# A two-layer hybrid block: the attention of a layer as a pipeline of steps, with the remaining merge-gate products cut in quarters and spread over the steps

## The chip, the core and the metric

One core of one Trainium2 chip runs the whole program. The metric is the device time of one execution in microseconds (us). The kernel before took 3766.13 us (median of three runs, 3756.99 to 3768.46). TensorE (PE) does the matrix products, VectorE (DVE) and ScalarE (ACT) the elementwise work, and the queue of SyncE (SP) issues nearly all DMAs.

## What is computed

Two layers over 1024 latent and 256 context tokens of width 1024. Each layer normalises the tokens, multiplies them by a wide input matrix, and feeds three mixers: a recurrence (branch A), a short convolution (B) and a differential attention (C). Their outputs are merged with sigmoid gates that are themselves products of the normalised input (`g_merge`). Cut to what matters here:

```python
def diff_attend(q, k, v, lam):                       # 4 heads, two 64-wide maps per head
    s = einsum('bqhcd,bkhcd->bhcqk', q, k) * (64 ** -0.5)
    p = softmax(s, axis=-1)
    attn = p[:, :, 0] - lam * p[:, :, 1]
    return einsum('bhqk,bkhv->bqhv', attn, v)

def merge_branches(y_a, y_b, y_c, z_a, z_b, z_c, g_merge, w_branch, w_out):
    y = stack([y_a * silu(z_a), y_b * silu(z_b), y_c * silu(z_c)], axis=-2)
    br = einsum('btiw,iwd->btid', y, w_branch)
    gates = sigmoid(g_merge.reshape(..., 3, 1024))
    return sum(gates * br, axis=-2) @ w_out
```

Latent queries read all 1280 keys, context queries only the 256 of the context. The last layer does not need the context's outputs, so there it has no context queries and no context gates.

## The kernel before

All products of projections are made in three parts of split precision: every operand is a high and a low half (`hT0h` and `hT0l` for the normalised tokens, `whi` and `wlo` for a weight block), and one term is three matmuls (`mm3`, L155). A *group* (`cm_group`, L165) is eight terms, so 24 matmuls into one PSUM tile `pjt`, for 128 output channels and 512 (or, for the context, 256) tokens.

A layer runs these stages in program order: the projections; the recurrence (`rwkv_stage`, L583; 20 chunks, each a serial chain of small products with DVE and ACT work between); the attention (`attn_stage`, L835); the branch products and the merge (`branch_stage`, L930); the output product. Three generators hold projection work that is not needed at once and serves as filling for PE: `vd_fill` (L795), `z_fill` (L806) and `g_fill` (L820), the last making the merge gates: 72 groups in layer 0 and 48 in layer 1, each followed by a tanh on ACT (`fth`) and a store (`th`). `fill` (L1143) is called 63 times in the recurrence, three times in a chunk and three ahead of them. `PACE` (L27) says in which of these calls one group is made: in each in layer 0, in two of three in layer 1. After the 29 and 26 groups of the first two generators, 38 gate groups are left in layer 0 and 32 in layer 1 when the recurrence ends. The program writes them behind the attention.

The order on each engine isn't that of the program. A list scheduler with a cost model places the instructions when the kernel is built, takes what is ready and comes first in the program, and takes later work where an engine would stand idle. So the gate groups written behind the attention lie between its instructions. On the chip each engine then works through its list in that fixed order.

The attention works on 128 queries at a time (`e` in 0, 1 of a block of 256, `qb`). Such a step makes scores `s` for two maps (six PSUM tiles from a pool of four), takes maxima on DVE (`mx`, L894) and exponentials on ACT (`p`, L903), scales and subtracts the second map (L911, L912), turns the result on PE (`at`, ten transposes, L918) and splits it into `ath` and `atl`. After two steps 30 matmuls make the output `o` of the block, which is copied (`oy`) and stored. Layer 0 has 40 steps (8 of them of context queries, with two key tiles in place of ten), layer 1 has 32.

`branch_stage` starts with the products of branch B: their operand `yb` (`yraw`, L1029) and their accumulators `acc` (loaded from the stored gates, L1044) lie in the buffers of `hT` (`bigh`, `bigl`), so they come free with the last gate group. Its other buffers (`bp`) lie where those of the attention were. The chain `y_a` (L946: loads `ra` and `rb`, then `pc`, `st`, logarithm, exponential, split into `ya`) must end before branch A's products on that token group. In layer 0 all products of the branches rotate over two more PSUM tiles (`PJB`, L26), which lie where the attention's were; in layer 1 only from the last of B's four weight blocks on.

Of the kernel before, what the change touches and what calls it, by code (L numbers as in the profile page):

```python
# [26 lines left out]
PACE = ((1, 1), (2, 3))  # L27
# [12 lines left out]
def tile_backbone(ctx: ExitStack, tc: tile.TileContext, xT_in, cond_in, w_mod, vecs, w_in, d_up, a_up,  # L40
# [114 lines left out]
    def mm3(ps, terms):  # L155
# [7 lines left out]
        return i.ins  # L163

    def cm_group(w, j, mov, t0, n):  # L165
        ps = pj_tile()
        terms = []
        for k in range(4 * len(w)):
            hi, lo = w[k // 4]
            s = slice(128 * j, 128 * j + 128)  # L170
            terms.append(((hi[:, k % 4, s], lo[:, k % 4, s]),
                          tok(mov, k, t0, n) if isinstance(mov, dict) else
                          (mov[0][:, k, t0:t0 + n], mov[1][:, k, t0:t0 + n])))
        run_late(mm3(ps[:, :n], terms))
# [620 lines left out]
    def vd_fill(l, b, sp):  # L795
# [6 lines left out]
        for i0 in range(0, 10, 2):  # L802
            tm_block(w, [i0], cb)
# [16 lines left out]
    def g_fill(l, sp):  # L820
        gq = GROUPS[l < NL - 1]
        for i in range(3):
            for b in range(4):
# [4 lines left out]
                for j, (t0, n) in jg:  # L828
                    p = cm_group(w, j, hT[0], t0, n)
# [5 lines left out]
    def attn_stage(l):  # L835
# [16 lines left out]
        for h in range(4):  # L852
            kd = []
            for c in range(2):
# [6 lines left out]
                kd.append((kh, kl))  # L861
            vh = ap.tile([128, 10, 128], F32R, tag="vh", name="vh")
# [5 lines left out]
            for qb in range(5 if full else 4):  # L868
                q0 = 256 * qb
                key0 = TL if q0 >= TL else 0  # L870
                nk = T - key0
                chunks = [(c, min(512, T - c)) for c in range(key0, T, 512)]
                nkt = nk // 128
                qraw = ap.tile([128, 2, 256], F32, tag="qraw", name="qraw", bufs=1)
                for c in range(2):
                    for e in range(2):
                        dma.dma_start(out=qraw[64 * e:64 * e + 64, c, :], in_=q_dr[l][h][64 * c:64 * c + 64, q0:q0 + 256])
                qs = ap.tile([128, 2, 256], F32R, tag="qs", name="qs", bufs=2)
                se.copy(out=qs, in_=qraw)
                ve.tensor_tensor(out=qs[64:128], in0=qraw[64:128], in1=qs[64:128], op=ALU.subtract)  # L880
# [379 lines left out]
```

## Time and profile before

| | us |
|---|---|
| median of three runs | 3766.13 |
| the profiled execution, as timed | 3755.48 |
| its span, first to last instruction | 3753.7 |
| PE busy | 3550.3 (95%) |
| DVE busy | 2403.3 (64%) |
| ACT busy | 1720.9 (46%) |
| mean granted TensorE clock | 0.977 |

A busy PE can be full, or it can be slow: matmuls overlap, and a matmul at half clock counts as busy for longer. So the number of matmuls in a stretch and the granted clock are read beside the busy time, and the stages are looked at one by one. The three lines of the program's timeline that matter here are the recurrence (747 to 1257 us in layer 0, 2605 to 3077 in layer 1), the attention (1272 to 1699 and 3092 to 3498), and the start of the branch stage after it.

### The profile page before, as it was taken

What the parts mean: (1) busy time and instruction counts of PE and PEld (TensorE: products, weight loads), DVE (VectorE), ACT (ScalarE), POOL (GpSimd) and SP (SyncE); (2) the same over time, 40 slices, a digit from 0 to 9 for tenths busy, and PEclk for the clock granted to TensorE, in tenths of its full rate; (3) what the DMA queues carried; (4) which work ended last, traced back from release to release, by engine and by line L of the source; (5) the groups of instructions that cost most, each with busy time, mean ns of one, the idle gap of its engine ahead of it and who ended that gap; (6) DMA issues with size and microseconds to landing.
All of it is one profiled execution on the core that took longest, in us unless ns stands there. A gap on an engine that the chain in (4) does not pass through costs nothing. (4 is left out here: it accounts for less than half of the span.)

```text
span 3753.7 us, 71161 instructions
## 1 busy us (share of the span) xinstructions
PE 3550.3 (95%) x28540; PEld 2917.8 (78%) x28540; DVE 2403.3 (64%) x5128; ACT 1720.9 (46%) x3295; POOL 82.9 (2%) x252
## 2 busy tenths in 40 slices
PE   7999999999999999968899999999999999999699
PEld 5788988888888788855776778988878778887377
DVE  6746733387777477765655766633898857778472
ACT  5644211144444477754434763212444436776440
POOL 0100000000000000000000110000000000000000
PEclk9999999999999999978999999999999999999799
DMA  5545222333332322405663455222333333233373
GB/s 203 143 129 157 77 95 94 132 105 106 116 107 99 103 89 86 151 21 171 212 199 128 117 156 157 80 96 93 106 112 119 114 94 100 84 98 100 129 244 124
DMA packets 378571, 454.75 MB, mean 121 GB/s; under 512 B 119808, under 2 KB 266752, under 8 KB 378240
## 3 DMA queue, kind: packets, MB, share of 16 engines
q1 hardware_dynamic: 376320, 447.58, 37.4%
q8 instruction: 224, 3.67, 0.4%
q0 software_dynamic: 1920, 2.62, 0.4%
q14 instruction: 107, 0.88, 0.1%
HBM read 300.66 MB, written 146.80 MB: 119 GB/s over the span
## 5 line engine op out<-in xcount | busy, mean ns | idle before, releaser
L160 PE MATMUL pjt<-hT0h,whi 128*128 128x512 f32 x1488 | 552.6, 372 | 3.6 <-ACT hT0h L292 1.4
L160 PE MATMUL pjt<-hT0l,whi 128*128 128x512 f32 x1488 | 536.4, 361 | 1.1 <-DVE hT0l L293 0.9
L160 PE MATMUL pjt<-hT0h,wlo 128*128 128x512 f32 x1488 | 530.9, 357 | 0.1
L160 PE MATMUL pjt<-hT1h,whi 128*128 128x512 f32 (+1 forms) x1072 | 422.3, 394 | 4.2 <-ACT tl L327 1.6
L160 PE MATMUL pjt<-hT1l,whi 128*128 128x512 f32 (+1 forms) x1072 | 417.0, 389 | 0.0
L160 PE MATMUL pjt<-hT1h,wlo 128*128 128x512 f32 (+1 forms) x1072 | 414.0, 386 | 1.3 <-DVE wlo L116 1.3
L115 ACT CAST whi<-wraw 128x1024 fp32r<-128x1024 f32 x208 | 217.2, 1049 | 301.0 <-PE pjt L160 274.2
L116 DVE TENSOR_TENSOR wlo<-wraw,whi 128x1024 fp32r<-128x1024 f32 x208 | 254.7, 1228 | 144.9 <-ACT whi L115 142.7
L160 PEld LDWEIGHTS pjt<-hT0h,whi 128*128 128x128 f32 x1488 | 283.0, 190 | 57.7 <-issue 10.2
L160 PEld LDWEIGHTS pjt<-hT0l,whi 128*128 128x128 f32 x1488 | 283.3, 190 | 43.9 <-issue 4.9
L160 PEld LDWEIGHTS pjt<-hT0h,wlo 128*128 128x128 f32 x1488 | 282.5, 190 | 42.4 <-issue 1.5
L903 ACT ACTIVATE p<-s,mx 128x512 f32<-128x512 f32 (+1 forms) x400 | 240.0, 610 | 90.1 <-DVE mx L898 84.8
L894 DVE TENSOR_REDUCE mx<-s 128x1 f32<-128x512 f32 (+1 forms) x400 | 228.1, 588 | 73.8 <-PE s L892 72.4
L160 PEld LDWEIGHTS pjt<-hT1h,whi 128*128 128x128 f32 x1072 | 202.0, 188 | 51.8 <-issue 7.3
L160 PEld LDWEIGHTS pjt<-hT1h,wlo 128*128 128x128 f32 x1072 | 201.9, 188 | 42.9 <-DVE wlo L116 2.8
L160 PEld LDWEIGHTS pjt<-hT1l,whi 128*128 128x128 f32 x1072 | 202.0, 188 | 41.8 <-issue 5.0
L892 PE MATMUL s<-kh,qs 128*128 128x512 f32 (+1 forms) x400 | 156.5, 397 | 38.6 <-ACT p L903 34.6
L645 ACT COPY dg<-mb 32x128 f32<-32x128 f32 x320 | 94.7, 296 | 161.8 <-DVE mb L639 143.6
L160 PE MATMUL pjt<-ya,whi 128*128 128x512 f32 (+1 forms) x448 | 144.1, 406 | 15.2 <-ACT ya L115 13.3
L892 PE MATMUL s<-kl,qs 128*128 128x512 f32 (+1 forms) x400 | 148.0, 375 | 1.2 <-DVE kl L116 1.2
L695 DVE TENSOR_TENSOR P<-at,R 128x16 f32<-128x16 f32 (+6 forms) x280 | 137.7, 492 | 9.0
L697 DVE TENSOR_REDUCE R<-P 128x4 f32<-128x16 f32 (+6 forms) x280 | 136.3, 487 | 8.6
(270 smaller groups left out, 7889.2 us busy)
## 6 DMA issues: line engine op xcount, KB each, us to landing
wraw<-in_w_in_dram SPq DMA_DIRECT2D x148, 512.0 KB, 3.9
kr<-kr SPq DMA_DIRECT2D x68, 512.0 KB, 4.4
wm<-in_w_mod_dram SPq DMA_DIRECT2D x48, 512.0 KB, 3.7
th<-fth SPq DMA_DIRECT2D x96, 256.0 KB, 2.1
wraw<-in_w_br_dram SPq DMA_DIRECT2D x36, 512.0 KB, 4.5
th<-th SPq DMA_DIRECT2D x64, 256.0 KB, 3.9
wraw<-in_w_out_dram SPq DMA_DIRECT2D x24, 512.0 KB, 4.3
bk<-bkt SPq DMA_DIRECT2D x80, 128.0 KB, 2.4
```

Of the source, the lines that this page charges most:

```text
L115: se.copy(out=hi, in_=src)
L116: ve.tensor_tensor(out=lo, in0=src, in1=hi, op=ALU.subtract)
L160: i = te.matmul(out=ps, lhsT=a, rhs=b, start=(c == 0), stop=(c == n - 1))
L645: se.copy(out=dg[s, d], in_=mb[s, d, p, :, 32 * q:32 * q + 32])
L695: ve.tensor_tensor(out=pv, in0=at[:, i0:i1, i1:32].unsqueeze(2).to_broadcast([128, 4, nm, n]), in1=R[:, b + 1:8, i1:32].unsqueeze(1).to_br ...
L697: ve.tensor_reduce(out=R[:, b + 1:8, i0:i1].rearrange("p m i -> p i m"), in_=pv, axis=AX.X, op=ALU.add)
L892: te.matmul(out=s[:, :n], lhsT=qs[:, c, 128 * e:128 * e + 128], rhs=kd[c][x][:, c0:c0 + n], start=(x == 0), stop=(x == 1))
L894: ve.tensor_reduce(out=mx[:, x0:x0 + 1], in_=s[:, :n], axis=AX.X, op=ALU.max)
L903: se.activation(out=p[:, o:o + n], in_=tiles[x0][:, :n], func=AF.Exp, scale=0.125, bias=mx[:, 3:4], accum_out=sums[:, x0:x0 + 1])
```

## The change

The attention is written as a pipeline of steps. In step x the scores and exponentials of step x's queries stand ahead of the turning of those of step x-1, and the output product of a block comes in the step after its second half was turned. The generators yield after each quarter of a group (`mm3_steps`), and the attention calls `fill(x, part)` twice in each step, which makes as many quarters as bring the total to an even share: 184 quarters over 41 slots in layer 0, 128 over 33 in layer 1. `PACE` in layer 0 goes from every turn of the recurrence to seven of eight, so 55 groups are made there in place of 63, and 46 gate groups are left for the attention in place of 38. In layer 1 the share stays at two of three, with other turns left out, and 32 groups remain as before.

```diff
-PACE = ((1, 1), (2, 3))
+PACE = ((7, 8, 46), (2, 3, 32))
...
+    def mm3_steps(ps, terms, step):
...
+            if c % (3 * step) == 0 and c < n:
+                yield
         last_mm[0] = i.ins
...
+    def cm_steps(w, j, mov, t0, n):
+
+        ps = pj_tile()
+        yield from mm3_steps(ps[:, :n], list(cm_terms(w, j, mov, t0, n)), 2)
+        run_late(last_mm[0])
+        yield ps[:, :n]
...
-                    p = cm_group(w, j, hT[0], t0, n)
+                    for p in cm_steps(w, j, hT[0], t0, n):
+                        if p is None:
+                            yield
...
-    def attn_stage(l):
+    def attn_stage(l, fill):
...
+        nq = 5 if full else 4
+        steps = [(h, qb, e) for h in range(4) for qb in range(nq) for e in range(2)]
+        kd = vd = qs = prev = done = None
+        for x, (h, qb, e) in enumerate(steps + [(0, 0, 0)]):
+            last = x == len(steps)
+            if not last:
+                if qb == 0 and e == 0:
+                    kd = keys(h)
+                if e == 0:
+                    qs = queries(h, qb)
+                sm = softmax(kd, qs, qb, e)
+                next(sm)
+            fill(x, 0)
+            if not last:
+                pr = next(sm)
+            if done is not None:
+                product(*done)
+                done = None
+            if prev is not None:
+                pp, ph, pq, pe = prev
+                if pe == 0:
+                    if pq == 0:
+                        vd = values(ph)
+                    at = [ap.tile([128, 10, 256], F32R, tag=t, name=t, bufs=1) for t in ("ath", "atl")]
+                turn(pp, at, pq, pe, 0)
+                fill(x, 1)
+                turn(pp, at, pq, pe, 1)
+                if pe == 1:
+                    done = (ph, pq, vd, at)
+            if not last:
+                prev = (pr, h, qb, e)
+        product(*done)
...
-        paced = itertools.count()
+        turns = itertools.count()
 
         def fill():
 
-            if next(paced) % PACE[l][1] < PACE[l][0]:
-                next(both, None)
+            x = next(turns)
+            if (x + 1) * PACE[l][0] // PACE[l][1] > x * PACE[l][0] // PACE[l][1]:
+                for _ in range(4):
+                    next(both, None)
...
-        attn_stage(l)
+        left = list(range(4 * PACE[l][2]))
+        slots = 8 * (5 if l < NL - 1 else 4) + 1
+
+        def fill_at(x, part):
+
+            want = (4 * PACE[l][2] * (2 * x + 1 + part)) // (2 * slots)
+            while 4 * PACE[l][2] - len(left) < want:
+                left.pop()
+                next(rest, None)
+
+        attn_stage(l, fill_at)
```

`keys`, `queries`, `values`, `softmax`, `turn` and `product` hold the code that stood in the loop before, with the same buffers; `softmax` pauses after the first map, `turn` makes eight transposes in its first part and two in the second.

What the scheduler makes of it is seen in the engines' lists. First PE in the last head of layer 0's attention (`s` are scores with the keys `kh` and `kl`, `at` transposes, `pjt` products of the filling). Before:

```order
L892 MATMUL s_16609<-kh_16335,qs_16533 128x512
L892 MATMUL s_16609<-kl_16336,qs_16533 128x512
L892 MATMUL s_16613<-kh_16335,qs_16533 128x256
L892 MATMUL s_16613<-kl_16336,qs_16533 128x256
L892 MATMUL s_16627<-kh_16342,qs_16533 128x512
L892 MATMUL s_16627<-kl_16343,qs_16533 128x512
L918 MATMUL at_16585<-cst_72,p_16553 128x128 x4
L918 MATMUL at_16592<-cst_72,p_16553 128x128 x4
L918 MATMUL at_16599<-cst_72,p_16553 128x128 x2
L892 MATMUL s_16631<-kh_16342,qs_16533 128x512
```

And now, in the same head:

```order
L161 MATMUL pjt_17790<-hT0h0_499,wlo_17781 128x512
L959 MATMUL at_17797<-cst_72,p_17574 128x128 x2
L926 MATMUL s_17811<-kh_17081,qs_17807 128x512
L926 MATMUL s_17811<-kl_17082,qs_17807 128x512
L926 MATMUL s_17815<-kh_17081,qs_17807 128x512
L926 MATMUL s_17815<-kl_17082,qs_17807 128x512
L161 MATMUL pjt_17790<-hT0h0_499,whi_17780 128x512
L926 MATMUL s_17819<-kh_17081,qs_17807 128x256
L926 MATMUL s_17819<-kl_17082,qs_17807 128x256
L161 MATMUL pjt_17790<-hT0l0_500,whi_17780 128x512
```

Gate products stand between the scores and the transposes here, where before there were none left; the transposes belong to the step before.

Then PE at the end of layer 1's attention (`bigl` and `bigh` are branch B's operand). Before, B's products stand between the scores:

```order
L160 MATMUL pjt<-bigh_36344,whi 128x512 x2
L160 MATMUL pjt<-bigh_36344,wlo 128x512
L892 MATMUL s<-kh,qs 128x512
L892 MATMUL s<-kl,qs 128x512
L160 MATMUL pjt<-bigh_36344,whi 128x512
L892 MATMUL s<-kh,qs 128x256
L892 MATMUL s<-kl,qs 128x256
```

Now the last gate products, the last two transposes and the last output product come first:

```order
L161 MATMUL pjt<-hT1h_20638,whi 128x512
L161 MATMUL pjt<-hT1l_20639,whi 128x512
L161 MATMUL pjt<-hT1h_20638,wlo 128x512
L959 MATMUL at<-cst,p 128x128 x2
L161 MATMUL o<-ath,vh 128x256
L161 MATMUL o<-atl,vh 128x256
L161 MATMUL o<-ath,vl 128x256
```

Before, all 192 matmuls of branch B's products in layer 1 stood ahead of the attention's last matmul; now 20 of them do, and the others follow it. In layer 0, 114 of them (78 of 512 and 36 of 256 columns) stood inside the attention, and now none. Gate matmuls between the first score of the attention and its last matmul: 551 of 512 and 288 of 256 columns before in layer 0, now 672 and 351; in layer 1 695 of 512 columns before, now 699.

Last the SP queue in layer 0, where the accumulators are loaded (in the trace these rows stand at 1573 to 1580 us). Before, among the last loads of queries and keys (`q_3`, `k_3`):

```order
L1044 DMA acc<-th_1_0_152 128x256
L877 DMA qraw<-q_3_111 64x256 x4
L1044 DMA acc<-th_1_1_153 128x256
L1044 DMA acc<-th_1_2_154 128x256
L1044 DMA acc<-th_1_3_155 128x256
L1044 DMA acc<-th_1_4_156 128x256
L1044 DMA acc<-th_1_5_157 128x256
L122 DMA wraw<-in_w_br_dram 128x1024
L857 DMA araw<-k_3_119 64x1280 x2
```

Now up to and past the last store of the attention (`o_3`), and ahead of the loads `ra` and `rb` with which `y_a` begins:

```order
L1119 DMA acc<-th_1_1_153 128x256
L858 DMA th_2_7_167<-fth 128x256
L969 DMA o_3_207<-oy 128x256
L1119 DMA acc<-th_1_2_154 128x256
L1104 DMA yraw<-y_2_198 128x256
L1104 DMA yraw<-y_3_199 128x256
L1119 DMA acc<-th_1_3_155 128x256
L1025 DMA ra<-yd_0_192 128x4x512
L1025 DMA rb<-yd_1_193 128x4x512
```

The accumulators' loads moved from among the transfers of the third and fourth head to the very end of the attention: twelve of them, 2.5 MB in sum, now stand in the queue's last rows ahead of `ra`. In layer 1 seven of 256 KB stand there.

## Rows read from the trace of the kernel before

**Rows 1.** The page: busy time, share of the span and instructions of each engine, and the granted TensorE clock in 40 equal slices of the span (tenths, 9 is 90% or more).

```profile
PE 3550.3 (95%) x28540; PEld 2917.8 (78%) x28540; DVE 2403.3 (64%) x5128; ACT 1720.9 (46%) x3295; POOL 82.9 (2%) x252
...
PEclk9999999999999999978999999999999999999799
```

**Rows 2.** Busy time by stretch in layer 0, from the first score of the attention into the branch stage: length, busy us and (instructions) of PE, of PE's weight loads, DVE, ACT and POOL, then the granted clock, the DMA share and GB/s.

```profile
1272.00:1300.00 28.00, 24.43 (x115) 19.38 (x116) 16.32 (x36) 14.77 (x34) 0.00 (x0) 0.94 0.48 130
1300.00:1550.00 250.00, 249.07 (x1465) 211.05 (x1464) 182.85 (x446) 176.80 (x412) 0.00 (x0) 1.00 0.27 83
1550.00:1612.00 62.00, 59.55 (x355) 50.15 (x353) 51.97 (x124) 44.46 (x102) 0.00 (x0) 1.00 0.61 189
1612.00:1698.80 86.80, 56.12 (x278) 43.87 (x279) 50.90 (x133) 47.64 (x118) 0.00 (x0) 0.72 0.03 10
1698.80:1795.00 96.20, 77.72 (x298) 54.15 (x297) 51.63 (x88) 48.82 (x71) 0.00 (x0) 0.88 0.52 177
```

**Rows 3.** The same for layer 1.

```profile
3092.00:3125.00 33.00, 31.21 (x145) 24.93 (x145) 22.18 (x49) 20.14 (x45) 0.00 (x0) 1.00 0.51 148
3125.00:3425.00 300.00, 298.91 (x1624) 246.09 (x1624) 227.01 (x516) 210.74 (x471) 0.00 (x0) 1.00 0.33 104
3425.00:3447.50 22.50, 22.34 (x119) 18.08 (x117) 17.51 (x43) 13.29 (x33) 0.00 (x0) 1.00 0.09 30
3447.50:3498.40 50.90, 35.96 (x188) 28.82 (x188) 27.52 (x69) 26.34 (x62) 0.00 (x0) 0.77 0.02 6
3498.40:3575.00 76.60, 46.00 (x106) 22.58 (x105) 33.96 (x53) 34.23 (x47) 0.00 (x0) 0.75 0.50 172
```

**Rows 4.** PE's groups by line and shape from 3125 to 3425 us (count; busy us, mean ns; idle before). The output product has three such rows of 124 or 125, the narrow scores two of 49; all other matmuls there have 512 columns.

```profile
L918 PE MATMUL at<-cst,p 128*128 128x128 f32 x250 | 36.4, 276 | 0.2
L160 PE MATMUL o<-atl,vh 128*128 128x256 f32 x125 | 35.3, 282 | 0.0
...
L892 PE MATMUL s<-kl,qs 128*128 128x256 f32 x49 | 14.4, 295 | 0.0
```

**Rows 5.** PE in order of time near the start of layer 0's attention: start, duration, engine, line, tiles, shape, count, and in brackets the idle time before and what ended it.

```profile
1284.07 0.28 PE L160 MATMUL pjt<-hT0l,whi 128*128 128x256 f32 x1
1284.19 0.28 PE L160 MATMUL pjt<-hT0h,wlo 128*128 128x256 f32 x1
1284.90 0.50 PE L892 MATMUL s<-kh,qs 128*128 128x512 f32 x1 [0.44 <-ACT p L903]
1285.24 0.39 PE L892 MATMUL s<-kl,qs 128*128 128x512 f32 x1
1287.95 0.39 PE L892 MATMUL s<-kh,qs 128*128 128x256 f32 x1 [2.33 <-ACT p L903]
...
1289.43 0.63 PE L160 MATMUL pjt<-hT0h,whi 128*128 128x512 f32 x1
...
1294.40 1.03 PE L918 MATMUL at<-cst,p 128*128 128x128 f32 x8
1295.19 0.48 PE L892 MATMUL s<-kh,qs 128*128 128x512 f32 x1
```

**Rows 6.** The same view in layer 0 where the filling has run out: the last matmul of it before 1696 us (a product of branch B), scores that waited, and the first matmul of two output products that follow each other.

```profile
1611.61 0.28 PE L160 MATMUL pjt<-bigh,wlo 128*128 128x256 f32 x1
...
1617.09 0.39 PE L160 MATMUL o<-ath,vh 128*128 128x256 f32 x1 [0.15 <-DVE mx L898]
...
1632.31 0.80 PE L892 MATMUL s<-kh,qs 128*128 128x512 f32 x1 [2.62 <-ACT p L903]
...
1637.79 0.80 PE L892 MATMUL s<-kh,qs 128*128 128x512 f32 x1 [2.97 <-ACT p L903]
...
1642.54 0.58 PE L160 MATMUL o<-ath,vh 128*128 128x256 f32 x1
```

**Rows 7.** PE's groups by line and shape from 1272 to 1698.8 us: the gate products of 512 and of 256 columns (three such rows each).

```profile
L160 PE MATMUL pjt<-hT0l,whi 128*128 128x512 f32 x184 | 73.2, 398 | 0.0
...
L160 PE MATMUL pjt<-hT0h,whi 128*128 128x256 f32 x96 | 27.5, 286 | 0.0
```

**Rows 8.** Busy time by stretch as in rows 2: the recurrence of layer 0, that of layer 1, and 50 us of layer 1's projections, where PE makes products of 512 columns and nothing else.

```profile
747.00:1257.00 510.00, 500.78 (x7377) 425.19 (x7377) 382.71 (x914) 209.93 (x448) 6.89 (x38) 1.00 0.31 104
2605.00:3077.00 472.00, 454.26 (x6917) 385.65 (x6917) 381.34 (x920) 204.53 (x434) 7.28 (x40) 1.00 0.34 111
...
2550.00:2600.00 50.00, 50.00 (x222) 41.40 (x221) 15.25 (x19) 8.15 (x11) 0.00 (x0) 1.00 0.16 58
```

**Rows 9.** The start of the chain `y_a` in order of time: the issue of `ra` on SP and the first sum on DVE, in layer 0 and in layer 1, and PE's wait in layer 1.

```profile
1701.30 0.57 SPq L950 DMA_DIRECT2D ra<-yd  x1
...
1709.61 2.50 DVE L957 TENSOR_TENSOR ra<-ra,rb 128x512 f32<-128x512 f32 x4 [1.54 <-DMA rb<-yd]
...
3501.15 0.57 SPq L950 DMA_DIRECT2D ra<-yd  x1
...
3511.96 2.50 DVE L957 TENSOR_TENSOR ra<-ra,rb 128x512 f32<-128x512 f32 x4 [10.91 <-DMA rb<-yd]
...
3512.75 2.04 PE L959 MATMUL pc<-ra,cst 128*128 128x512 f32 x2 [14.04 <-DMA rza<-za]
```

**Rows 10.** DMA issues by line over the whole run: count, KB each, median us from issue to landing.

```profile
acc<-th SPq DMA_DIRECT2D x32, 256.0 KB, 5.0
...
rb<-yd SPq DMA_DIRECT2D x4, 1024.0 KB, 7.6
```

More of the change, by code (lines that the diff above doesn't have):

```diff
@@ L153, in run_mm @@
                 order.enter_context(tc.issue_after(i.ins))
-    def mm3(ps, terms):
+    def mm3_steps(ps, terms, step):
         n = 3 * len(terms)
@@ L802, in vd_fill @@
         for i0 in range(0, 10, 2):
-            tm_block(w, [i0], cb)
+            ps = pj_tile().rearrange("p (e f) -> p e f", e=2)
+            for e in range(2):
+                terms = [(tok(hT[0], k, (i0 + e) * 128, 128), (w[k // 4][0][:, k % 4, :], w[k // 4][1][:, k % 4, :]))
+                         for k in range(8)]
+                yield from mm3_steps(ps[:, e, :], terms, 4)
+                if e == 0:
+                    yield
+            run_late(last_mm[0])
+            cb(ps, i0)
             yield
@@ L828, in g_fill @@
                 for j, (t0, n) in jg:
-                    p = cm_group(w, j, hT[0], t0, n)
+                    for p in cm_steps(w, j, hT[0], t0, n):
+                        if p is None:
+                            yield
                     th = sp.tile([128, 512], F32, tag="fth", name="fth", bufs=FTH)
@@ L851, in attn_stage, with keys @@
         nlam = lm[:, 3:4]
-        for h in range(4):
+        def keys(h):
             kd = []
@@ L861, in attn_stage, with values @@
                 kd.append((kh, kl))
+            return kd
+        def values(h):
             vh = ap.tile([128, 10, 128], F32R, tag="vh", name="vh")
@@ new lines, in values, with queries @@
+            return vh, vl
+        def queries(h, qb):
+            q0 = 256 * qb
+            qraw = ap.tile([128, 2, 256], F32, tag="qraw", name="qraw", bufs=1)
+            for c in range(2):
+                for e in range(2):
+                    dma.dma_start(out=qraw[64 * e:64 * e + 64, c, :], in_=q_dr[l][h][64 * c:64 * c + 64, q0:q0 + 256])
+            qs = ap.tile([128, 2, 256], F32R, tag="qs", name="qs", bufs=2)
+            se.copy(out=qs, in_=qraw)
+            ve.tensor_tensor(out=qs[64:128], in0=qraw[64:128], in1=qs[64:128], op=ALU.subtract)
+            return qs
@@ new lines, in turn @@
+        def turn(pr, at, qb, e, part):
+            nkt = 2 if qb == 4 else 10
+            for k0 in range(0, nkt, 4):
+                if (k0 < 8) != (part == 0):
+                    continue
+                m = min(4, nkt - k0)
+                pt = pst.tile([128, 4, 128], F32, tag="at", name="at")
+                for k in range(m):
+                    te.transpose(out=pt[:, k, :], in_=pr[:, 128 * (k0 + k):128 * (k0 + k) + 128], identity=ident)
+                o = slice(128 * e, 128 * e + 128)
+                split(at[0][:, k0:k0 + m, o], at[1][:, k0:k0 + m, o], pt[:, :m, :])
@@ new lines, in product @@
+        def product(h, qb, vd, at):
+            kt0, nkt = (8, 2) if qb == 4 else (0, 10)
+            po = pst.tile([128, 256], F32, tag="at", name="o")
+            mm3(po, [((vd[0][:, kt0 + k, :], vd[1][:, kt0 + k, :]), (at[0][:, k, :], at[1][:, k, :])) for k in range(nkt)])
+            y = ap.tile([128, 256], F32, tag="oy", name="oy", bufs=1)
+            se.copy(out=y, in_=po)
+            dma.dma_start(out=o_dr[l][h][:, 256 * qb:256 * qb + 256], in_=y)
+        nq = 5 if full else 4
+        steps = [(h, qb, e) for h in range(4) for qb in range(nq) for e in range(2)]
```

118 lines of the change are left out of this document (50 added, 68 removed).

## The prediction

> **What bounds the kernel now.** I read the page first. PE is busy 95% of the span, DVE 64%, ACT 46%, so PE is the bound on average, and the granted clock shows two dips in 40 slices, one in the middle and one close to the end [rows 1]. An average hides where it isn't the bound, so next come the tables by stretch. In the dense part of the attention PE is full at full clock: 300 us of layer 1 with 298.91 us busy and 1624 matmuls, 250 us of layer 0 with 249.07 and 1465 [rows 2, 3]. In the last 86.8 us of layer 0's attention PE makes 278 matmuls at a clock of 0.72; in the last 50.9 us of layer 1's 188 at 0.77 [rows 2, 3]. These are the two dips. The rows in order of time say why: after 1611.61 us no filling is left, scores wait 2.62 and 2.97 us for a score tile that ACT's exponentials release, and two output products, one for each two steps, start at 1617.09 and 1642.54 us, 25.45 us apart [rows 6]. So the attention without filling runs at 12.7 us per step by its own chain scores, maximum, exponential, subtraction, transposes, and with filling it is PE that sets the pace. Behind both attentions is a second chain: `y_a` can't load `ra` before the attention's buffers are free, `ra` is issued 2.5 to 3 us after its end, the first sum is ready some 11 to 13 us after it, PE waits 14.04 us in layer 1 [rows 9], and from 3498.4 to 3575 us it makes only 106 matmuls, at 0.75 [rows 3].
>
> **Prices.** Busy time of overlapping matmuls is longer than what they cost, so I take counts. A pure stream of 512 columns makes 222 in 50 us: 0.225 us each [rows 8]. Two successive products of 256 columns start 0.12 us apart, and eight transposes take 0.79 us to the next start, 0.10 each [rows 5]. In the 300 dense us there are 250 transposes, 374 output matmuls and 98 narrow scores [rows 4], which leaves 902 of 512 columns: (299 - 472 x 0.12 - 250 x 0.10) / 902 = 0.241 us. 374 / 30 is 12.5 pairs of steps, 24.06 us per pair; DVE's 227.01 us are 18.2 per pair, ACT's 210.74 are 16.9 [rows 3, 4].
>
> **Term 1, layer 1's attention.** By the order lists it now holds 719 products of 512 columns (699 of gates, 20 of branch B), 256 wide scores, 128 narrow ones, 480 output matmuls and 320 transposes: 975 x 0.241 + 608 x 0.12 + 320 x 0.10 = 340 us. The start stays: 145 matmuls in the first 33 us where the dense rate makes 179, so 6 us [rows 3]. For new stalls I take 0.3 us in each of 32 steps, 10 us. The bounds of that: 0.04 us per step, as the dense stretch had (1.09 us idle in 25 steps) [rows 3], and 2.33 us, the wait of a score at the attention's start [rows 5]. I stay near the first since the mixture there is the same as now; not at it, since a pair then had (902 - 200) / 12.5 = 56 products beside it and now has 44, which leaves 21.6 us of PE for DVE's 18.2 or less. 340 + 6 + 10 = 356 against 406.3 from 3092.2 to the end at 3498.5: **50 us saved**. What makes this up is 172 products of branch B that move behind the attention (41 us) and 20 us of the tail, less the stalls. The moved products cost nothing only under cover: the 76.6 us behind the attention hold 106 matmuls, 24 us at 0.225, so 52 us are free for 41 [rows 3]; without cover the saving is some 10 us.
>
> **Term 2, layer 0's attention.** 672 and 351 gate products, 256 wide and 160 narrow scores, 504 output matmuls, 336 transposes: 928 x 0.241 + 1015 x 0.12 + 336 x 0.10 = 379 us. The start: 115 matmuls in 28 us where the rate of 1465 in 250 makes 164, so 8 us [rows 2]. Stalls as above, 40 x 0.3 = 12. Sum 399 against 426.6: **27 saved**, with 7.6 groups more inside than before. The 114 branch-B products that move out are 23 us, and go into 96.2 us that hold 298 matmuls, some 60 us at 0.2, so 36 are free [rows 2].
>
> **Term 3, layer 0's recurrence.** Eight groups leave it, 7.6 of which the lists show in the attention. Two gate groups in three have 512 columns and one 256, as their counts of 184 and 96 show [rows 7]: 24 x (2 x 0.225 + 0.12) / 3 = 4.56 us per group, 34.7 in all. Not all comes back, as a turn without filling waits for its own chain: layer 1's recurrence, with a third of its turns empty, has PE idle 3.8%, layer 0's with none 1.8% [rows 8]. An eighth empty gives 2.5%, 4 us more; I take 6, since the empty turn's DVE work (382.71 us [rows 8]) gets denser. **28 saved**, between 10 and 35.
>
> **Term 4, the start of the branches.** On SP the accumulators' loads now stand right ahead of `ra` and `rb`, and what is queued behind them is the chain `y_a`, for which DVE and PE wait. An `acc` of 256 KB lands 5.0 us after its issue, `rb` 7.6 [rows 10]; the stretches with these loads move 172 to 177 GB/s [rows 2, 3]. 2.5 MB in layer 0 are at most 14 us of that, 1.8 MB in layer 1 at most 10; they wait for the last gate products' reads, so part of it starts earlier. Nothing, if all land in time, and 24 us are the ends. I take **8 us lost** in both layers, since the last gate product stands a step ahead of the end and branch B's products now cover PE meanwhile.
>
> The list's bookkeeping (new pauses of the generators, other buffers of filling) adds no instruction to the engines.
>
> **A rule that speaks against it.** At the start of layer 0's attention PE stands idle for 2.33 us before a score that waits for ACT, while gate products that need nothing from it come after it, at 1289.43 us [rows 5]: what is ready doesn't pass what waits. The Trainium skill, "TensorE: Matmul & The Clock Gate", section "Step-by-step: what each phase is for", says the same as a rule: "The MATMULs themselves stay in program order", and only weight loads are pulled ahead. The trace agrees; were it otherwise, the stalls of terms 1 and 2 would be nil and the sum 119 instead of 97. The filling helps only where it stands ahead of the waiting matmul, and its place was chosen when the program was built. That is the second rival.
>
> **Rivals.** *The attention keeps its own pace.* If 12 to 12.7 us per step is DVE's and ACT's chain and not PE's or the latency of one step, terms 1 and 2 are nil, and 28 - 8 = 20 us remain: 3746. For it: 24.06 and 25.45 us per pair with and without filling are close together [rows 4, 6]. Against it: DVE's 18.2 and ACT's 16.9 us per pair, some of which is the filling's own, leave room at 21.6; the tail waits for what one step's chain does in a row, and the pipeline puts the next step's scores into that. *The head of the queue.* Every step's scores take six tiles from a pool of four, so each step has a place where PE can meet a score whose tile isn't free. If the list, made ahead of time, misjudges this by as much as [rows 5] show, each of 72 steps pays 2.33 us: 168 us against the 22 of my sum, 146 more, **3815, slower by 49**. It decides from (97 + 22) / 72 = 1.65 us per step on. Against it: the dense stretch was made by the same means and loses 0.04. *The change doesn't do what it says*, the filling running out early as before: the lists show gate products up to the last transposes of both layers, so only 2 in 100; that would be about no change. *Better than the sum*, with stalls and loads at nothing: 97 + 22 + 8 = 127, 3639, and a little below if the recurrence gives all.
>
> **How the numbers follow.** 50 + 27 + 28 - 8 = 97 us. The profiled execution took 3755.48 us, so 3658; the median of three runs lies 10.65 above that execution, so on the medians 3669. The range: stalls of 1 us per step in place of 0.3 cost 50, term 3 at its low end 18, which together make 3737; loads at their bound cost 16. Upward to 3740, downward to 3635, 8 in 10. The attention at its own pace 8 in 100, just beyond the range; the head of the queue 6; below the range 4; no effect 2. About 0.3% (11 us, what a measurement of this kernel can tell from no change) is 3755 to 3777: faster takes the forecast, what lies below it and half of the first rival, 0.88; within, the rest of that rival and no effect, 0.06; slower 0.06.
>
> **What would show it.** Gate products up to the last step of both attentions, and no stretch at their ends with a clock of 0.7; layer 1's attention at about 356 us, layer 0's at 399, output products 21 to 22 us apart; layer 0's recurrence near 482 us; the first sum of `ra` not later than some 16 us after the attention's end, and the 172 products of branch B done while `y_a` is made. Output products still 24 to 25 us apart with PE waiting for ACT's `p` would show the first rival; idle time of about 2 us ahead of one score in each step, with gate products behind it, the second; a `y_a` that begins 10 us later, or a stretch behind the attention longer by what was moved there, that term 4 or the cover was wrong. Then 3669 is wrong by that much.

## The result, and the profile after

The changed kernel took 3643.56 us (median of four runs, 3640.67 to 3645.92) against 3765.41 of the kernel before on the same chips: a ratio of 0.9679, 95% interval 0.9662 to 0.9697, 122 us less. The prediction was 3669, with a range of 3635 to 3740. Its profiled execution took 3640.67 us with a span of 3638.9, against 3753.7 before: 114.8 us, and the profile accounts for these. The other 7 lie in the executions: the profiled one of before took 9.9 us less than its median, that of the changed kernel 2.9 less.

The page of the changed kernel, the lines that answer to [rows 1]:

```profile
PE 3516.8 (97%) x28540; PEld 2915.3 (80%) x28540; DVE 2394.9 (66%) x5128; ACT 1714.8 (47%) x3295; POOL 84.9 (2%) x252
...
PEclk8999999999999999999999999999999999999999
```

The instructions of these engines are the same in number. Both dips of the clock are gone, and PE's idle time fell from 203.4 us (3753.7 - 3550.3) to 122.1.

Busy time by stretch in layer 0 of the changed kernel, from the first score into the branch stage, with columns as in [rows 2]; the fourth line is the attention's last 42 us:

```profile
1252.00:1280.00 28.00, 27.51 (x146) 22.81 (x147) 22.44 (x48) 20.03 (x45) 0.00 (x0) 1.00 0.61 174
1280.00:1530.00 250.00, 248.58 (x1506) 214.23 (x1506) 197.49 (x496) 188.83 (x453) 0.00 (x0) 1.00 0.26 80
1530.00:1592.00 62.00, 62.00 (x371) 53.27 (x370) 48.91 (x118) 46.51 (x113) 0.00 (x0) 1.00 0.25 82
1592.00:1634.10 42.10, 42.08 (x263) 37.53 (x262) 28.12 (x69) 28.79 (x63) 0.00 (x0) 1.00 0.39 128
1634.10:1730.30 96.20, 84.81 (x378) 63.54 (x377) 57.17 (x98) 50.56 (x75) 0.00 (x0) 1.00 0.62 208
```

And in layer 1, to be read beside [rows 3]:

```profile
3035.70:3069.00 33.30, 31.22 (x139) 25.00 (x140) 22.73 (x48) 20.78 (x45) 0.00 (x0) 0.95 0.54 155
3069.00:3326.00 257.00, 256.77 (x1456) 213.79 (x1454) 215.37 (x522) 203.93 (x476) 0.00 (x0) 1.00 0.26 82
3326.00:3377.20 51.20, 50.59 (x291) 42.54 (x290) 38.51 (x86) 37.33 (x82) 0.00 (x0) 1.00 0.30 96
3377.20:3453.80 76.60, 71.72 (x278) 50.91 (x277) 45.90 (x69) 37.57 (x50) 0.00 (x0) 1.00 0.66 225
```

The ends of both attentions now hold as many matmuls per us as their middle (263 in 42.1 us, 1506 in 250), at a clock of 1.00. The last line of each table is the stretch behind the attention, as long as in [rows 2, 3]: 378 matmuls in place of 298, 278 in place of 106, also at 1.00.

Where the stages begin and end is read from the first and last start of a tile's instructions. For the changed kernel, the scores and output products of both layers (minimum, median and maximum duration in ns, then first and last start in us):

```profile
L926 PE MATMUL s<-kh,qs x208: 274/391/505, 1252.0 to 1624.2; 128*128 128x512 f32 x64, 128*128 128x256 f32 x40
...
L161 PE MATMUL o<-ath,vl x168: 274/283/287, 1283.9 to 1634.1; 128*128 128x256 f32 x168
...
L926 PE MATMUL s<-kh,qs x192: 274/394/628, 3035.7 to 3360.5; 128*128 128x512 f32 x128, 128*128 128x256 f32 x64
...
L161 PE MATMUL o<-ath,vl x160: 274/283/287, 3072.2 to 3377.2; 128*128 128x256 f32 x160
```

So the attentions take 1634.1 - 1252.0 = 382.1 and 3377.2 - 3035.7 = 341.5 us. The same reading for all kernels of this study gives the table on which the rest stands. The recurrence counts from its first `dg` (a copy on ACT) to the attention's first score, "between" from the end of layer 0's attention to layer 1's first `dg`, "end" from the end of layer 1's attention to the last instruction. All in us, from one profiled execution each; the median is of the timed runs.

| kernel | median | recurrence 0 | attention 0 | between | recurrence 1 | attention 1 | end |
|---|---|---|---|---|---|---|---|
| before | 3765.4 | 532.5 | 426.6 | 919.3 | 474.1 | 406.0 | 255.5 |
| changed | 3643.6 | 513.2 | 382.1 | 926.5 | 475.1 | 341.5 | 261.7 |
| changed_again | 3650.6 | 507.0 | 382.5 | 929.0 | 482.5 | 340.1 | 262.1 |
| pipeline_alone | 3650.5 | 513.1 | 344.8 | 976.4 | 475.9 | 328.6 | 273.9 |
| spread_alone | 3731.3 | 511.5 | 426.2 | 920.0 | 480.1 | 396.1 | 255.4 |
| pace_of_before | 3641.6 | 532.7 | 354.4 | 932.5 | 477.3 | 339.6 | 263.5 |
| whole_groups | 3641.2 | 507.0 | 383.5 | 932.4 | 474.7 | 338.4 | 260.7 |
| product_at_once | 3663.5 | 511.8 | 388.4 | 930.4 | 474.9 | 358.5 | 253.7 |
| more_filling | 3702.7 | 483.4 | 421.5 | 928.9 | 471.4 | 391.9 | 264.2 |
| own_pace_new | 3997.2 | 509.6 | 361.8 | 1137.8 | 474.5 | 334.0 | 439.5 |
| own_pace_old | 4161.6 | 532.3 | 445.1 | 1105.9 | 475.9 | 422.1 | 439.1 |
| empty_turn_later | 3645.6 | 507.1 | 382.0 | 931.8 | 479.1 | 339.6 | 265.3 |
| empty_turns_later_both | 3645.6 | 507.8 | 382.7 | 932.9 | 475.7 | 340.3 | 262.3 |

### The profile page after: what moved, and what is told of

Same layout as the page of the kernel before. It is cut to its first block, busy times and chain, and to the rows that moved or that the text cites. A ratio compares the mean times of both kernels' runs of the same rounds, so it can differ in the third digit from the quotient of the medians.

```text
span 3638.9 us, 71231 instructions
## 1 busy us (share of the span) xinstructions
PE 3516.8 (97%) x28540; PEld 2915.3 (80%) x28540; DVE 2394.9 (66%) x5128; ACT 1714.8 (47%) x3295; POOL 84.9 (2%) x252
## 4 chain that ended last, share of the span: by engine, by line
PE 69%; DVE 17%; ACT 6%; issue 4%; DMA 4%; SPq 0%; DVEq 0%; ACTq 0%; POOL 0%; POOLq 0%
PE pjt L161 48%; PE s L926 4%; PE o L161 3%; PE at L959 2%; PE X L151 2%; DVE P L709 2%; PE pa L151 1%; PE U L151 1%; DVE R L711 1%; DVE wlo L116 1%; DVE mb L653 1%; PE Y L151 1%; DVE P L713 1%; DVE R L715 1%; PE D L151 1%
## 5 line engine op out<-in xcount | busy, mean ns | idle before, releaser
L161 PE MATMUL pjt<-ya,whi 128*128 128x512 f32 (+1 forms) x448 | 136.6, 389 | 6.8 <-ACT ya L115 5.7
```

## The experiments

Theory 1 was: PE at full clock sets the attention's pace once the pipeline is there, and a product costs the same in whatever covered place it stands. Its rivals were that the even spread makes the gain, and the two of the prediction (the attention's own pace, the head of PE's queue).

**The pipeline alone.** `attn_stage` gets a filling that does nothing; the gate products are written behind the attention, as in the kernel before.

```diff
-        attn_stage(l, fill_at)
+        attn_stage(l, lambda x, part: None)
```

> The pipeline of steps without the even spread: nothing is called in the attention, the gate products are written behind it, and the order made ahead of time pulls them in where PE would idle. The lists show what this does: layer 1 nearly the same as in the changed kernel (656 gate products inside in place of 699), layer 0 only 528 and 269 in place of 672 and 351, about 44 us of PE less inside. Theory 1 (PE sets the attention's pace, and filling that is spared there only moves behind it): layer 0's attention 338 us if PE alone binds it, layer 1's 331, with the branch stage longer by about what left, so within 15 us of the changed kernel's 3643. Theory 2 (the even spread is what makes the gain): the steps with little filling fall back to 12 us each, layer 0's attention stays near 382 or above, and the total is 25 to 45 us longer.

3650.46 us, 0.9703 of the kernel before (0.9681 to 0.9724), an interval that overlaps with that of the whole change. Theory 1 holds: with less filling inside, layer 0's attention took 344.8 us, not 382 (338 were expected), so nothing falls back to 12 us per step. Busy time by stretch: most of layer 0's attention, its end, and the stretch behind it, where the gate products that were left come:

```profile
1282.00:1532.00 250.00, 247.97 (x1499) 211.65 (x1498) 212.09 (x536) 203.73 (x489) 0.00 (x0) 1.00 0.28 84
...
1575.00:1599.20 24.20, 24.20 (x160) 21.21 (x160) 17.00 (x47) 16.42 (x41) 0.00 (x0) 1.00 0.22 77
1599.20:1660.00 60.80, 58.15 (x306) 49.96 (x305) 14.52 (x17) 14.48 (x21) 0.00 (x0) 1.00 0.51 169
```

PE is full up to the end without any spreading by hand: the order made when the kernel was built distributes the filling itself when the steps need less of it. What layer 0's attention gave, 37.3 us, the stretch behind it took back and 12.6 more ("between" is 976.4 in place of 926.5), with DVE at 14.52 of 60.8 us there. The four timed executions run from 3640.6 to 3655.8 us and the profiled one is the longest of them, so whether the spread is worth a few us can't be told from these runs.

**The even spread alone.** The steps in the order of the kernel before, with the two calls for filling in each.

```diff
             fill(x, 0)
-            if not last:
-                pr = next(sm)
...
+            pr = next(sm)
+            turn(pr, at, qb, e, 0)
+            fill(x, 1)
+            turn(pr, at, qb, e, 1)
+            if e == 1:
+                product(h, qb, vd, at)
+        fill(len(steps), 1)
```

> The even spread without the pipeline: in each step the transposes follow that step's own exponentials, as in the kernel before, with the quarters written into the same two places. The lists still hold all of branch B's products inside the attention (114 in layer 0, 191 in layer 1), since a step that waits for its own chain takes more filling. Theory 1 (two gains: no slow tail, which the spread brings, and branch B's products moved under the cover of y_a, which needs the pipeline): layer 0's attention about 410 us, layer 1's about 385, the branch stages some 6 us shorter each, total near 3698. If the pipeline brings nothing of its own, the total is that of the changed kernel, 3643. If the spread brings nothing, it stays at 3740 or above.

3731.33 us, 0.9922 (0.9904 to 0.9939), where theory 1 had 3698. It was worse than that: the attentions took 426.2 and 396.1 us, not 410 and 385. Against the kernel before, layer 0's recurrence gave 21.0 us and layer 1's attention 9.9, of which layer 1's recurrence took 6.0 back; layer 0's attention holds 7.6 groups more in the same time. So this run's gain is mostly the recurrence's, through the new share of layer 0, which it has too; whether the spread was needed to take the 7.6 groups in isn't tried. Both attentions still end slowly. The last 37.6 us of layer 0's, and the last 43.8 of layer 1's:

```profile
1640.00:1677.60 37.60, 29.02 (x159) 24.36 (x158) 21.56 (x59) 20.05 (x50) 0.00 (x0) 0.77 0.02 7
```

```profile
3430.00:3473.80 43.80, 35.27 (x186) 28.02 (x185) 26.19 (x63) 23.11 (x54) 0.00 (x0) 0.88 0.05 16
```

The spread writes filling up to the last step, but the order moves ready products ahead to wherever a step waits, takes branch B's as well (114 and 191 of them stand inside), and runs out before the end. Beside the run before, where nothing was spread and PE was full to the end, this says that it isn't the spread that brings the filling to the end but steps that ask for less.

**Layer 0's old share.** `PACE` of layer 0 back to every turn, 38 groups left.

```diff
-PACE = ((7, 8, 46), (2, 3, 32))
+PACE = ((1, 1, 38), (2, 3, 32))
```

> The change with layer 0's old share: a group in every turn of the recurrence, 38 gate groups for the attention in place of 46. Term 3 by itself: the recurrence of layer 0 is longer by 18 to 28 us. If PE alone sets the attention's pace at this smaller filling too, the attention is shorter by 8 groups, 35 us, to about 347 us, and the total is 10 to 15 us better than the changed kernel's 3643. If DVE's and ACT's chain sets the pace from there on (DVE has about 297 us of work in layer 0's attention), the attention stops near 360 to 370 us and the total is equal or up to 10 us worse.

3641.55 us, 0.9681 (0.9662 to 0.97): the same as the whole change. The recurrence is 19.5 us longer, the attention 27.7 shorter, the stage behind it 6.0 longer. Neither expectation for the attention was met: it took 354.4 us, between the 347 of a full PE and the 360 to 370 of DVE's chain, with PE idle for 5.3 us of it. The change's new share neither gains nor loses.

**Whole groups.** The shares rounded down to groups of 24 products.

```diff
-            while 4 * PACE[l][2] - len(left) < want:
-                left.pop()
-                next(rest, None)
+            while 4 * PACE[l][2] - len(left) < want // 4 * 4:
+                for _ in range(4):
+                    left.pop()
+                    next(rest, None)
```

> The change with whole groups in place of quarters: the same shares, rounded down to groups of 24 products (5.4 us of PE in one place). If stalls at the head of PE's queue are what the quarters avoid, a step whose transposes stand behind a whole group makes the next scores late: 0.5 to 1 us per step, 35 to 70 us longer than 3643. If PE is full in any case, as the trace of the changed kernel shows it, the time is the same within 6 us.

3641.23 us, 0.9683 (0.9661 to 0.9704), the same. The quarters aren't needed. But the run doesn't test what whole groups in one place would cost, since the scheduler splits them by itself. In the trace the filling of layer 0's attention stands in 158 unbroken stretches, against 164 in the changed kernel (144 and 150 in layer 1); the longest has 32 products in both, and 306 of 1023 products stand in stretches of 20 or more, against 123. In this run too scores come between the products of a group:

```profile
3278.49 0.40 PE L161 MATMUL pjt<-hT1l,whi 128*128 128x512 f32 x1
3278.72 0.39 PE L926 MATMUL s<-kh,qs 128*128 128x512 f32 x1
3278.95 0.39 PE L161 MATMUL pjt<-hT1h,wlo 128*128 128x512 f32 x1
```

That the head of PE's queue is no cost here is seen from idle time: in the whole attention PE is idle for 1.9 us in layer 0 and 2.9 in layer 1 of the changed kernel, and 2.2 and 2.8 in this one.

**The pace without filling.** The remaining products are held behind the attention's last output product, in the changed kernel (with the empty filling of the first run) and likewise in the kernel before. One execution each.

```diff
-        for _ in rest:
-            pass
+        with tc.issue_after(last_mm[0]):
+            for _ in rest:
+                pass
```

> The pipeline with no filling at all: the remaining gate products are held behind the last output product of the attention (the same work in sum). It shows the pace at which the attention runs by itself. If the pipeline takes the latency of a step's chain away, DVE binds: it has 276.6 us of work in layer 1's attention of the changed kernel, some of it the filling's, so 17 to 18 us per pair of steps, 280 to 300 us for layer 1's attention. If the chain of DVE and ACT were the attention's own pace (the first rival of the prediction), it stays at 24 to 25 us per pair, about 400 us. The total is far above 3643 in both cases, since 46 and 32 groups follow uncovered.

> The kernel before, likewise with all filling held behind the attention. From its tail, 25.45 us per pair: 16 pairs and 6 us of start are 413 us for layer 1's attention, and 430 to 440 for layer 0's. If the tail was slow only for its clock and not for its chain, less than 380 for layer 1.

The attention of layer 1 took 334.0 us with the pipeline and 422.1 without: 20.9 and 26.4 us per pair of steps over the 16 pairs, the start included. The old one is near what was expected, the new one between the two expectations: above the 280 to 300 that DVE's work would allow, and far below 400. Busy time of 257 us of layer 1's attention in the one and in the other:

```profile
3255.00:3512.00 257.00, 192.57 (x954) 149.63 (x954) 203.94 (x511) 187.67 (x450) 0.00 (x0) 0.81 0.14 40
```

```profile
3331.60:3588.60 257.00, 162.96 (x740) 122.99 (x739) 161.18 (x397) 147.67 (x346) 0.00 (x0) 0.69 0.11 31
```

And what PE waited for there, from its groups by line: with the pipeline,

```profile
L926 PE MATMUL s<-kh,qs 128*128 128x512 f32 x156 | 75.8, 486 | 38.9 <-ACT p L936 34.3 <-ACT kh L115 4.2
...
L959 PE MATMUL at<-cst,p 128*128 128x128 f32 x253 | 53.0, 357 | 20.4 <-DVE p L947 8.1 <-DVE mx L931 7.5 <-DVE sums L945 3.2
```

and without:

```profile
L892 PE MATMUL s<-kh,qs 128*128 128x512 f32 (+1 forms) x120 | 66.7, 560 | 67.7 <-ACT p L903 66.4 <-ACT kh L115 1.2
...
L918 PE MATMUL at<-cst,p 128*128 128x128 f32 x200 | 40.7, 352 | 21.4 <-DVE atl L116 9.3 <-DVE mx L897 6.7 <-DVE p L912 5.4
```

The wait of scores for a tile that ACT's exponentials release falls from 66.4 us to 34.3 in the same 257 us, while 954 matmuls are made in place of 740. DVE is busy 79% of the time and not full: a part of the chain stays, at a clock of 0.81.

**The output product at once.** Right behind its block's transposes, in place of a step later.

```diff
-                    done = (ph, pq, vd, at)
+                    product(ph, pq, vd, at)
...
-        product(*done)
         es.close()
```

> The change with the output product of a block right behind its transposes, in place of one step later; the scores still stand a step ahead. The lists show 86 products of branch B back inside layer 1's attention, so it waits more. If only the scores' place counts, layer 1's attention is 340 us plus those 86 products (19 us) and the total the same as the changed kernel's within 10 us. If the wait of the product for the last split is what a step can't cover, each of the 16 pairs in layer 1 and 20 in layer 0 loses 1 to 2 us: 35 to 70 us longer than 3643.

3663.52 us, 0.9742 (0.9727 to 0.9756), 20 us above the changed kernel. It lies between the two expectations (within 10 us, and 35 to 70). Layer 1's attention took 358.5 us, 17.0 more, as with 86 products of branch B inside it (the trace has these 86; they give 8 us back behind it). Layer 0's took 388.4, 6.3 more with the same filling, and PE is idle there for 5.7 us in place of 1.9. The delay of the product is a small part of the pipeline's gain of more than 100.

**More filling in the attention.**

```diff
-PACE = ((7, 8, 46), (2, 3, 32))
+PACE = ((3, 4, 54), (1, 2, 43))
```

> The change with more filling moved out of the recurrences: three of four turns in layer 0 (54 groups left for the attention in place of 46), one of two in layer 1 (43 in place of 32). With PE full in the attention each group costs there what it costs anywhere: layer 0's attention 36 us longer, layer 1's 59. The recurrences give back a part: term 3 measured 19 us for 8 groups, so 19 and 27 by that rate. Total 3643 + 95 - 46 = 3692. If the recurrence gave back all that PE had in those turns, it would stay at 3643; if it gave nothing, 3738.

3702.70 us, 0.9851 (0.9834 to 0.9867), where 3692 was expected. Layer 0 pays 39.4 us in the attention for 8 groups and gets 29.8 back (23.6 beside the second execution of the changed kernel); layer 1 pays 50.4 for 11 and gets 3.7. The attention's side is about as theory 1 had it in layer 0 (36) and cheaper in layer 1 (59), with PE idle for less than 1 us in either; the recurrence's in layer 1 isn't (27 expected). 468 us of layer 1's recurrence show what stands behind it:

```profile
2550.00:3018.00 468.00, 424.19 (x6521) 356.33 (x6520) 373.43 (x914) 192.92 (x412) 7.20 (x40) 0.95 0.31 100
```

PE is busy 424.19 us at 0.95 and so idle for 43.8, against 17.7 of 472 us in the kernel before [rows 8]: with a group in every other turn it is mostly not PE that sets this recurrence's pace. That it runs by its own chain from there on, near 471 us, is the reading nearest to hand; no run with still less filling tried it.

**Where the empty turns stand.** In the changed kernel's profile the clock fell to 0.66 from 760 to 780 us, behind the recurrence's first, empty turn. I took this dip for what term 3 fell short of, moved the empty turns, and ran the changed kernel again beside (no edit).

```diff
-            x = next(turns)
+            x = next(turns) + (4 if l == 0 else 0)
```

> The change with the empty turns of layer 0's recurrence shifted by four, so that the fifth turn of each eight is empty and not the first; the number of groups stays 55. In the changed kernel the granted clock is 0.66 from 760 to 780 us, just after the first, empty turn, and only 158 matmuls are made there, where the kernel before made 214 at 1.00. If this dip is why term 3 came out as 19 us and not 28, the time from the recurrence's start to the attention's first score falls from 513 to about 505 us, and the total by 6 to 9 us beside the changed kernel run again. If any empty turn costs the same wherever it stands, both stay.

The second run has `(4, 1)[l]` in place of the bracket, which moves layer 1's as well.

> The same, and in layer 1 the empty turn is the third of each three and not the first, as in the kernel before. Layer 1's recurrence took the same with either order (474.1 us to the first score before, 475.1 after), so nothing more than the run above is expected, within 3 us; if the place of its first empty turn counted too, 3 to 8 us more.

> The changed kernel as it is, run again beside the two others: 3643 us, and the dip of the clock near 770 us again in its profile if it belongs to the kernel's order and not to one execution.

3645.56 us (0.968, 0.9667 to 0.9694), 3645.59 (0.9678, 0.9662 to 0.9693) and 3650.57 (0.9698, 0.9681 to 0.9716): all the same, so where the empty turns stand gains nothing that can be measured in the total. Layer 0's recurrence did take 507.1 us in place of 513.2, near the 505 expected, but so did the changed kernel in its second execution. These 20 us in the changed kernel, in its second execution, and with the empty turn later:

```profile
760.00:780.00 20.00, 17.63 (x158) 16.52 (x160) 13.00 (x37) 6.76 (x15) 0.36 (x2) 0.66 0.05 15
```

```profile
760.00:780.00 20.00, 16.82 (x254) 15.27 (x253) 17.63 (x43) 9.69 (x19) 0.36 (x2) 1.00 0.19 52
```

```profile
760.00:780.00 20.00, 17.52 (x202) 16.23 (x200) 16.42 (x43) 7.00 (x15) 0.36 (x2) 0.83 0.08 27
```

The same program has the dip in one execution and not in the other, and the recurrence takes 513.2 and 507.0 us. Ahead of it PE waits for DVE, 2.69 us in both executions; the 32 matmuls behind the wait take 1.92 us in the first and 1.08 in the second:

```profile
762.37 1.92 PE L151 MATMUL U<-xs,tt 32*32 32x64 f32 x32 [2.69 <-DVE tt L717]
```

```profile
763.71 1.08 PE L151 MATMUL U<-xs,tt 32*32 32x64 f32 x32 [2.69 <-DVE tt L717]
```

Whether the empty turn makes the dip stays open. In the six other kernels whose first turn is empty, all of which have this wait or one like it, the clock of these 20 us is 0.66 (pipeline_alone, spread_alone), 0.74 (product_at_once, own_pace_new), 0.84 (more_filling) and 0.91 (whole_groups). With the turn moved it is 0.83 in both runs, and without an empty turn (before, own_pace_old, pace_of_before) 1.00 in all three, where the same wait is 1.04 us or less. With 55 groups, the recurrence takes 509.6 to 513.2 us where that clock is 0.74 or lower, and 507.0 to 507.8 where it is 0.83 or higher, so a deep dip goes with some 3 to 6 us. It keeps company with the empty turns but doesn't follow from them alone. Layer 1's recurrence has such dips as well: it took 482.5 us in the second execution of the changed kernel, with 0.87 and 0.93 in two of its stretches (2560 to 2600 and 2650 to 2700 us), and 475.1 in the first, with 1.00 there.

## Why the prediction was right, and what it had wrong

Direction and cause were right: the tails without filling are gone, and PE is full at full clock through both attentions, and at full clock behind them. By terms, from the profiled spans:

| term | predicted | measured |
|---|---|---|
| 1, layer 1's attention | -50 | -64.5 |
| 2, layer 0's attention | -27 | -44.5 |
| 3, layer 0's recurrence | -28 | -19.3 |
| 4, the start of the branches | +8 | +13.4 |
| layer 1's recurrence, and the time ahead of layer 0's | 0 | +0.1 |
| sum | -97 | -114.8 |

The sum came nearer than its terms: 1 and 2 gave 32.0 us more than forecast, 3 and 4 14.1 less, and that these partly cancel is luck.

**Terms 1 and 2** were mis-sized at the stalls. I had 0.3 us in each of 72 steps, 22 us in all; there are none beyond the start. The prices were good, as four shares of filling in layer 0 show, with the counts of the order lists at 0.241, 0.12 and 0.10 us:

| kernel | gate and branch-B products, 512 and 256 columns | price, us | measured | excess |
|---|---|---|---|---|
| pipeline_alone | 528 and 269 | 334.5 | 344.8 | 10.3 |
| pace_of_before | 555 and 288 | 343.3 | 354.4 | 11.1 |
| changed | 672 and 351 | 379.0 | 382.1 | 3.1 |
| more_filling | 816 and 408 | 420.6 | 421.5 | 0.9 |

The start alone was to cost 8. The excess isn't idle time: PE is idle for 4.1, 5.3, 1.9 and 0.7 us in these four attentions, start included. In layer 1 the same prices are less good: 3.8 us too low for pipeline_alone, 6.4 for the changed kernel, 5.4 too high for more_filling (957 gate products). One count was wrong besides: of layer 1 I said that 20 products of branch B stay inside the attention. None do, the first of them follows the last output product, and 191 in place of 172 moved behind the attention:

```profile
3377.23 0.28 PE L161 MATMUL o<-ath,vl 128*128 128x256 f32 x1
3377.35 0.63 PE L161 MATMUL pjt<-bigl,whi 128*128 128x512 f32 x2
```

Without these 20 the price of layer 1 is (699 + 256) x 0.241 + 73 + 32 = 335 us, and 335 + 6 for the start is 341, against the 341.5 measured. The end that I took for the stalls' lower bound, the dense stretch with 1.09 us idle in 300 [rows 3], was the value itself. The reason that I gave for staying off it, less filling in a pair, speaks the other way: the steps need less. With the stalls at nothing my sum was 119 us, which I gave as the saving of a PE that lets ready products pass a waiting one. That the saving is near it says nothing about such a PE: with some 2 to 3 us of idle time in an attention there is hardly a wait left to pass, and [rows 5] still show one that wasn't passed.

**Term 3** is 19.3 us in this execution and 25.5 in the second one of the same kernel (532.5 - 507.0), so between the ends given and, in the second, close to 28. The dip of the clock goes with the difference; why one execution has it stays open.

**Term 4** has the right order of size and mostly the wrong cause. The loads hardly delay `y_a`: the first sum of `ra` stands 13.4 us behind the attention's end in layer 0 and 13.7 in layer 1, against 10.8 and 13.8 before [rows 9], so 2.6 us later in layer 0 and no later in layer 1. The rows on DVE, layer 0 and then layer 1:

```profile
1647.48 2.50 DVE L1032 TENSOR_TENSOR ra<-ra,rb 128x512 f32<-128x512 f32 x4 [1.51 <-DMA rb<-yd]
```

```profile
3390.92 1.29 DVE L1032 TENSOR_TENSOR ra<-ra,rb 128x512 f32<-128x512 f32 x2 [0.39 <-DMA rb<-yd]
```

The rest of the cost is read as cover that doesn't reach. In layer 0 the 96.2 us behind the attention take 378 matmuls in place of 298, so 80 of the 114 that were moved there; the other 34 at 0.2 are 7 us, and "between" is 7.2 longer. In layer 1 the 76.6 us take 172 more (278 in place of 106) where 191 were moved; the other 19 at 0.225 are 4 us of the 6.2 by which the end is longer. That this accounts for it is counted, not tried, and in layer 0 it leaves no room for the 2.6 us of delay: no run here moved the branch products alone.

**The rivals.** The attention at its own pace is refuted: with less filling layer 0's attention runs in 344.8 us in pipeline_alone, where this rival had it stay near 426, and without any filling a pair of layer 1 takes 20.9 us in place of 26.4. The old pace was latency, in part at the low clock, and not work: at 26.4 us per pair DVE and ACT were busy for 161.18 and 147.67 of 257 us. The head of PE's queue is refuted by the idle time: 1.9 us in the 40 steps of layer 0 and 2.9 in the 32 of layer 1, where this rival had 2.33 in each step; whole_groups, which was to try it, changed PE's order too little to add much. The filling reached the end, as the lists had it. Beyond the prediction, the runs took the change apart: the pipeline alone gives the whole gain within what these runs can tell (0.9703 against 0.9679 and 0.9698), the quarters, their even spread and the new share in layer 0 give none that can be told from nothing, and the spread without the pipeline 0.8%, most of it in layer 0's recurrence through the new share. No run has the pipeline with neither the spread nor the new share.

No run points to a version beyond the changed kernel: shares to both sides, whole groups and other empty turns end at 3641 to 3651 us or above.

## What to carry to other kernels

When an engine looks full in the middle of a stage and starved at its end, don't ask first how the filling is distributed but how much each step consumes only to hide its own latency; a step with less latency makes the same filling last, and a list scheduler then spreads it unaided. Once the engine is full, moving filling between stages moves time one for one, less what the giving stage returns: measure that return (24 to 30 of 39.4 us in one recurrence, 3.7 of 50.4 in the other) before shifting shares. If a scheduler orders the instructions, look at the engine's order before you take a run for a test of where the products stand. And products that lose their place under one wait need another whose free time is counted: 80 of 114 and 172 of 191 fitted here.

## What the runs showed of the hardware

A stage without filling can be slower than the same stage with it. Layer 0's pipelined attention took 361.8 us with none, and 344.8 with 528 and 269 products inside (pipeline_alone); layer 1's took 334.0 and, with 656 inside, 328.6. 250 us of the first, beside the 247.97 busy us at 1.00 shown above for pipeline_alone:

```profile
1275.80:1525.80 250.00, 185.44 (x914) 142.83 (x914) 194.73 (x505) 177.88 (x436) 0.00 (x0) 0.79 0.16 44
```

PE was idle a quarter of the time, the granted clock was 0.79, and the chain's own scores took longer. In layer 1 the mean score without filling (both widths) takes 486 ns at 0.81, in the groups by line above; in the same group of the changed kernel, from 3069 to 3326 us at 1.00, it takes 392:

```profile
L926 PE MATMUL s<-kh,qs 128*128 128x512 f32 x153 | 60.0, 392 | 0.2
```

That the low clock is the whole of the difference isn't tried by itself, and the run without filling is one execution. The prediction knew the low clock of the tails [rows 2, 3], but not that filling can give back more than its own time.
